# Gate products 44 steps later, sums of expert numbers on ScalarE, banks 4 and 4

## The chip, the cores and the metric

One core of a Trainium2 chip runs the kernel. The metric is the device time of one execution in microseconds (us). TensorE multiplies matrices, VectorE, ScalarE and GpSimd (POOL in the profile) work on 128 partitions at once, SyncE (SP) issues loads, and 16 DMA engines move the data. Each engine takes its own instructions in the order in which they were written out, and waits on semaphores for the others.

## The reference, cut to what matters

A decoder block on 512 tokens of 1024 features. A mixer (pooling heads, gating heads, one output projection) gives `x`. Then comes the expert part, for each token:

```python
s1, i1 = top_k(scores of key half 0, 16);  s2, i2 = top_k(scores of key half 1, 16)   # 8 heads
cv, ci = top_k(s1[:, None] + s2[None, :], 16)
expert = i1[ci // 16] * 128 + i2[ci % 16]            # 8 heads x 16 = 128 experts of 16384
gate   = softmax(cv)
act    = gelu(h2 . peer_u[expert])                   # 128 numbers
out    = sum over the 128 of gate * act * peer_v[expert]
```

The result is `rmsnorm(x + out)`.

## The kernel before, in words

The tokens are four tiles of 128. The *search* for expert numbers runs in groups A (tile 0), B (tile 1) and C (tiles 2 and 3), head by head: `q_unit` and `score` on TensorE, `top_keys` and `top_pairs` on VectorE, `numbers` on POOL (it multiplies a 0/1 mask with the candidate numbers into the tile `ml`, 50 candidates x 16 picks, one buffer per pool), and `collect`, which sums `ml` over the 50 candidates into `ef`, one nonzero each, and for A and B copies the 16 numbers to `eG`. Group C has two tiles in one `ml`.

Tiles 0 and 1 are then computed by *gather steps*: 512 steps (`g_step`), 128 over rows of `peer_u` and 128 over rows of `peer_v` for each of the two tiles. POOL issues an indirect DMA of 128 rows (0.5 MB, tile `ga`, NG = 6 buffers), VectorE multiplies: L401 forms a dot product per token into `actG`, L408/L410 add a weighted row. After 64 steps of the first kind ScalarE takes the Gelu of 64 columns (L404) and VectorE multiplies with the gates (L405) at once.

Tiles 2 and 3 are computed densely by TensorE over all 16384 experts: 128 `u_block`s (a block of `uT`, 0.5 MB, read by SyncE into five `raw` buffers; 16 matmuls into a PSUM bank "act"; evacuated by ScalarE with Gelu, L703, into `gl`), then 128 `v_block`s, which add into four banks over the rows of `peer_v`. In between the gates are spread over the experts: `hot_pieces` (VectorE), `spread` (TensorE) and `weigh` (VectorE) for two halves of 32. PSUM has eight banks: six named "bank" and two "act".

At the end `x_load` reads `norm_final` and the rows of x back into the room of the first `gl`, `total` adds, ScalarE sums squares, and `finish` normalizes and stores, once for each tile.

The order of all this is made by a planner in Python before anything is issued: `Plan.run` keeps a clock for each engine, and gives it the ready item of the lowest `prio`; an item has a cost in us and dependences with a delay. What `q_unit`, `score` and `u_block` ask of ScalarE is written out together with their TensorE item. Gather steps come when the list PACE allows, at prio 2 when they are due (one per SLOW us until SLOW_UNTIL, with `due` counted on from the first step) and at prio 4 otherwise; the search of A, B, C on VectorE has prio 1, 1.5 and 3. The planned times fix only the order of each engine's instructions; nothing waits for a clock on the chip.

Of the kernel before, what the change touches and what calls it, by code (L numbers as in the profile page):

```python
# [8 lines left out]
F32 = mybir.dt.float32  # L9
BF16 = mybir.dt.bfloat16  # L10
I32 = mybir.dt.int32
U32 = mybir.dt.uint32
AF = mybir.ActivationFunctionType
OP = mybir.AluOpType
# [4 lines left out]
P = 128  # L19
# [25 lines left out]
C_MM = 0.86  # L45
C_Q0, C_Q1, C_U, C_V, C_SMM = 2.1, 5.4, 3.43, 3.43, 1.5
C_HOT, C_MUL, C_GAT = 2.2, 0.72, 1.31
PACE = ((0.0, 1.85), (570.0, 2.12), (800.0, 1.98), (840.0, 2.12), (1050.0, 1.98), (1270.0, 1.4))
SLOW, SLOW_UNTIL = 2.9, 570.0
SLACK, SLIP, LAG = 8.0, 10.0, 6.0  # L50


# [93 lines left out]
def hybrid_block(ctx, tc, A):  # L146
# [4 lines left out]
    def bcast(ap, n):  # L151
        return bass.AP(tensor=ap.tensor, offset=ap.offset, ap=[[0, P], [1, n]])
# [9 lines left out]
        return keep.tile(shape, dt, name=name)  # L162

    def bank(shape):
        return psum[-1].tile(shape, F32, name="bank", bufs=6 if len(psum) > 1 else 3)

    def side_bank(shape, name, n):
        return psum[0].tile(shape, F32, name=name, bufs=n)
# [82 lines left out]
    def qt(shape, dt, name, **k):  # L251
        return mp.tile(shape, dt, name=name, **k)
# [2 lines left out]
    keysT = qt([P, 2, P], F32, "keysT")  # L255
    ident = qt([P, P], F32, "ident")
    iock = qt([P, NCAND, TOPK], BF16, "iock")
    ef, cv = {}, {}
    for g in "AB":
        ef[g] = qt([P, 1, HEADS, TOPK], F32, "ef" + g)  # L260
# [97 lines left out]

    def collect(g, h):
        ml = sums.pop((g, h))  # L360
        V.tensor_reduce(ef[g][:, :, h], ml.rearrange("p t c k -> p t k c"), AX.X, OP.add)  # L361
        if g != "C":
            V.tensor_copy(eG[:, TILES[g][0], h * TOPK:(h + 1) * TOPK], ef[g][:, 0, h])

    def softmax(g, gate):
        qt, n = kq(g), len(TILES[g])
# [20 lines left out]
    def gather(k):  # L387
# [2 lines left out]
        G.indirect_dma_start(out=ga[k], out_offset=None, in_=A["peer_v" if v else "peer_u"],  # L390
                             in_offset=bass.IndirectOffsetOnAxis(ap=eG[:, t, col:col + 1], axis=0))

    def g_step(k):
        while gissued[0] < min(k + NG, NSTEP):
            gather(gissued[0])
            gissued[0] += 1
        g = ga.pop(k)
        t, v, col = place(k)
        c = actG[:, t, col:col + 1]
        if not v:  # L400
            V.scalar_tensor_tensor(scr, g, 1.0, h2nat[t], op0=OP.mult, op1=OP.mult, accum_out=c)  # L401
            if col % HALF == HALF - 1:
                cs = slice(col + 1 - HALF, col + 1)
                S.activation(actG[:, t, cs], actG[:, t, cs], AF.Gelu)  # L404
                V.tensor_mul(actG[:, t, cs], actG[:, t, cs], gG[:, t, cs])  # L405
        elif col == 0:
            xe[t] = keep.tile([P, D], F32, name="h2n%d" % t)
            V.tensor_scalar(xe[t], g, c, None, op0=OP.mult)  # L408
        else:
            V.scalar_tensor_tensor(xe[t], g, c, xe[t], op0=OP.mult, op1=OP.add)  # L410
# [264 lines left out]
    gl, gp1, late = [None, None], [], {}  # L675

    def act_bank(shape):
        return psum[-1].tile(shape, F32, name="act", bufs=2)

    def switch():  # L680

# [115 lines left out]

    xr = {}

    def x_load():  # L800
        room = gp1[0].tile([P, HALF, GW], F32, name="gl1").rearrange("p a w -> p (a w)")
        for k, t in enumerate(("g", 0, 1, 2, 3)):
            xr[t] = room[:, k * D:(k + 1) * D]
            nc.scalar.dma_start(xr[t], bcast(A["norm_final"], D) if t == "g" else xd[t])

    def total(t):
        y = xr[t]
# [23 lines left out]
    def search(g, q, extra, prio):  # L831

        n = len(TILES[g])
        sc, tk, tp, nb, co = [], [], [], [], []
        for h in range(HEADS):
            sc.append(add("pe", 0.6 * n, lambda h=h: score(g, h), [(q[2 * h + 1], 0.8)] + extra, 2))
        back = 1 if g == "C" else 2
        for h in range(HEADS):
            tk.append(add("dve", 3.1 * n, lambda h=h: top_keys(g, h),
                          [(sc[h], 0.8)] + tp[-1:] + (nb[h - 2:h - 1] if h > 1 else []), prio))  # L840
            tp.append(add("dve", 2.6 * n + 0.2, lambda h=h: top_pairs(g, h),
                          [tk[-1]] + (nb[h - back:h - back + 1] if h >= back else []), prio))
            nb.append(add("pool", 1.5 + 1.5 * n, lambda h=h: numbers(g, h),
                          [(tp[-1], LAG)] + co[-1:], 1))
            co.append(add("dve", 1.5 * n + 0.1, lambda h=h: collect(g, h), [(nb[-1], 2.0)],
                          prio - 0.2))
        return sc, co, co[-1]

    q0 = []
# [26 lines left out]
    for r in range(2):  # L876
        hots, spreads, weighs = [], [], []
        for q in range(GW // SG):
            deps = hots[-1:] + spreads[-2:-1] + [us[(r + 1) * HALF - 1], late_item]
            if r:  # L880
                deps += [us[-1], sc[0][-1]]
            for cost, fn in hot_pieces(r, q):
                hots.append(add("dve", cost, fn, deps, 1.9))
                deps = hots[-1:]
            deps = [(hots[-1], SLACK)] + spreads[-1:] + [(w, 4.0) for w in weighs[-2:-1]]
            spreads.append(add("pe", C_SMM, spread, deps, 1))
            weighs.append(add("dve", C_MUL, weigh, [(spreads[-1], 2.0)] + weighs[-1:], 1.8))
        sc[r] = weighs
# [14 lines left out]
        marks[n] = Item("dve", 0.0, None)  # L903
        return marks[n]

    xl = add("act", 0.3, x_load, [(vs[HALF], 2.0)], 1)
    for t, last in enumerate((steps_end(2 * P), steps_end(4 * P), vs[-1], vs[-1])):
        tot = add("dve", 1.4, lambda t=t: total(t), [(last, 0.3), (xl, 15.0)], 1.5)
        add("dve", 2.4, lambda t=t: finish(t), [(tot, 1.4)], 1.6)
# [66 lines left out]
```

## Time and profile before

| | |
|---|---|
| median of 3 runs | 1350.66 us (1347.7 to 1353.95) |
| profiled execution, its own time | 1349.46 us |
| its span, first to last instruction | 1347.7 us |
| mean granted TensorE clock | 0.966 |
| moved by DMA | 455.99 MB, mean 338 GB/s |

The span is that of the recorded instructions; 1.76 us of the execution lie around it. Busy times are shares of the span; idle time of an engine that isn't the bottleneck costs nothing. In a timeline, the bracket behind a row is the engine's idle time before it and what ended it.

### The profile page before, as it was taken

The page shows a single profiled execution, that of the slowest core. Times are in us where ns is not written, and L with a number is a line of the kernel's source. Part 1 is how long each engine was busy: PE and PEld are TensorE (multiplying, and loading weights), DVE is VectorE, ACT ScalarE, POOL GpSimd, SP SyncE. Part 2 cuts the span into 40 slices and gives each one's busy share as a digit, 9 for nine tenths or more (in the row PEclk, how much of TensorE's full clock was granted, in tenths as well). Part 3 has the DMA queues.
Part 4 walks back from the last instruction along what each step waited for, and adds up shares of the span by engine and source line. Part 5 has one row for each costly group of instructions (what it writes and reads, how often), then busy time and mean ns, then how long its engine had stood idle before and what let it go on. Part 6 is the DMA issues. An engine that isn't in the chain of part 4 may idle for free.

```text
span 1347.7 us, 17430 instructions
## 1 busy us (share of the span) xinstructions
PE 1249.9 (93%) x5998; PEld 843.3 (63%) x5998; DVE 1083.0 (80%) x2432; ACT 136.0 (10%) x314; POOL 701.2 (52%) x762
## 2 busy tenths in 40 slices
PE   6999986999999999999999997999999998999980
PEld 3485542899888888788888884544444443444430
DVE  2267887899899993799999996999999847566577
ACT  2311321111211111201010000000000000000001
POOL 0023376645776662755655664555656535444452
PEclk9999988999999999999999999999999999899995
DMA  9767269936799997899999999999999999999994
GB/s 348 277 228 261 81 216 399 349 103 210 276 383 357 369 350 266 331 372 381 386 400 358 400 349 410 353 382 392 404 372 406 391 410 367 406 409 410 409 383 183
DMA packets 127784, 455.99 MB, mean 338 GB/s; under 512 B 14288, under 2 KB 16720, under 8 KB 127696
## 3 DMA queue, kind: packets, MB, share of 16 engines
q0 software_dynamic: 74304, 270.57, 52.5%
q1 hardware_dynamic: 52240, 180.12, 35.6%
q10 hardware_dynamic: 1152, 4.19, 0.8%
q8 instruction: 47, 0.77, 0.2%
q14 instruction: 41, 0.34, 0.1%
HBM read 450.63 MB, written 4.19 MB: 337 GB/s over the span
## 4 chain that ended last, share of the span: by engine, by line
DMA 26%; PE 25%; DVE 19%; issue 18%; POOL 10%; ACT 1%; SPq 0%; POOLq 0%; DVEq 0%; another core or an unknown queue 0%; ACTq 0%
DMA ga<-peer_v,eG 18%; PE act L204 15%; POOL ga L390 8%; PE bank L204 8%; DMA ga<-peer_u,eG 7%; DVE h2n L410 5%; DVE scr L401 3%; DVE og L767 2%; DVE ob L762 1%; DMA raw<-w_in 1%; DVE gl L796 1%; PE g L204 1%; PE pb L204 1%; DVE oa L771 1%; DVE efA L361 1%
## 5 line engine op out<-in xcount | busy, mean ns | idle before, releaser
L204 PE MATMUL bank<-raw,gl 128*128 128x512 f32 x1024 | 452.6, 601 | 6.3 <-DMA raw<-peer_v 6.3
L204 PE MATMUL act<-h2T,raw 128*128 128x256 f32 x2048 | 452.5, 381 | 3.4 <-ACT gl L703 2.9
L390 POOL DMA_INDIRECT ga<-peer_v,eG x256 | 288.8, 1128 | 264.7 <-DVE h2n L410 180.8
L204 PEld LDWEIGHTS act<-h2T,raw 128*128 128x128 f32 x2048 | 387.3, 191 | 56.6 <-ACT gl L703 3.7
L390 POOL DMA_INDIRECT ga<-peer_u,eG x256 | 304.6, 1190 | 205.6 <-DVE scr L401 146.8
L410 DVE SCALAR_TENSOR_TENSOR h2n<-ga,actG,h2n 128x1024 f32<-128x1024 f32 x254 | 326.3, 1284 | 105.9 <-DMA ga<-peer_v,eG 100.6
L401 DVE SCALAR_TENSOR_TENSOR scr<-ga,h2n 128x1024 bf16<-128x1024 f32 x256 | 318.9, 1246 | 40.8 <-DMA ga<-peer_u,eG 34.8
L204 PEld LDWEIGHTS bank<-raw,gl 128*128 128x128 f32 x1024 | 194.3, 192 | 240.9 <-issue 233.0
L703 ACT ACTIVATE gl<-act 128x256 f32<-128x256 f32 x128 | 49.0, 384 | 419.0 <-PE act L204 355.8
L204 PE MATMUL pb<-raw,xs 128*128 128x512 f32 x192 | 86.7, 607 | 2.3 <-ACT gu L500 1.2
L204 PEld LDWEIGHTS <-ob 128*128 128x128 bf16 x1536 | 56.1, 98 | 37.7 <-issue 18.2
L356 POOL TENSOR_TENSOR ml<-eq,ce 128x800 f32<-128x800 bf16 (+1 forms) x24 | 49.2, 2049 | 55.0 <-DVE efA L361 29.9
L767 DVE TENSOR_TENSOR og<-oa,gT 128x512 bf16<-128x512 bf16 x192 | 73.7, 421 | 2.2
L204 PEld LDWEIGHTS pb<-raw,xs 128*128 128x128 f32 x192 | 37.0, 196 | 46.6 <-issue 42.7
L204 PE MATMUL bank<-h2T,raw 128*128 128x256 f32 x256 | 57.9, 379 | 0.0
L204 PEld LDWEIGHTS bank<-h2T,raw 128*128 128x128 f32 x256 | 47.4, 190 | 5.8
L762 DVE TENSOR_TENSOR ob<-iota,abT 128x1024 bf16<-128x1024 bf16 x64 | 43.9, 686 | 0.4 <-remote 0.4
L204 PE MATMUL g<-raw,xs 128*128 128x512 f32 x64 | 32.8, 657 | 10.5 <-DMA raw<-w_in 10.5
L204 PE MATMUL act<-og,ob 128*128 128x64 bf16 x768 | 30.6, 196 | 9.5 <-DVE og L767 6.8
L327 POOL TENSOR_TENSOR ce<-xf 128x8 f32<-128x8 f32 (+8 forms) x168 | 36.8, 253 | 2.0
L609 POOL DMA_DIRECT2D xd<-x x4 | 2.4, 608 | 62.1 <-DVE x L604 62.0
L204 PE MATMUL bank<-og,ob 128*128 128x64 bf16 x768 | 29.4, 193 | 4.3 <-DVE og L767 3.7
(173 smaller groups left out, 780.9 us busy)
## 6 DMA issues: line engine op xcount, KB each, us to landing
raw<-uT SPq DMA_DIRECT2D x128, 512.0 KB
raw<-peer_v SPq DMA_DIRECT2D x128, 512.0 KB
raw<-w_q SPq DMA_DIRECT2D x32, 512.0 KB
raw<-w_in SPq DMA_DIRECT2D x23, 512.0 KB
raw<-w_out SPq DMA_DIRECT2D x16, 512.0 KB
ga<-peer_u,eG POOLq DMA_INDIRECT x256
ga<-peer_v,eG POOLq DMA_INDIRECT x256
x<-x SPq DMA_DIRECT2D x4, 512.0 KB
```

The costliest lines, as they stand in the source:

```text
L204: T.matmul(out, l, r, start=start, stop=stop)
L327: eng.tensor_tensor(ov, av, bv, op=OP.add)
L356: G.tensor_tensor(ml, eq, ce[:, :, :, None].to_broadcast(sh), op=OP.mult)
L361: V.tensor_reduce(ef[g][:, :, h], ml.rearrange("p t c k -> p t k c"), AX.X, OP.add)
L390: G.indirect_dma_start(out=ga[k], out_offset=None, in_=A["peer_v" if v else "peer_u"], in_offset=bass.IndirectOffsetOnAxis(ap=eG[:, t, col ...
L401: V.scalar_tensor_tensor(scr, g, 1.0, h2nat[t], op0=OP.mult, op1=OP.mult, accum_out=c)
L410: V.scalar_tensor_tensor(xe[t], g, c, xe[t], op0=OP.mult, op1=OP.add)
L703: S.activation(gl[r][:, i], b, AF.Gelu)
L762: V.tensor_tensor(tl["b"], iota2[:, None].to_broadcast(sb), col(abT[:, 1, t]).to_broadcast(sb), op=OP.is_equal)
L767: V.tensor_tensor(tl[k], tl["a"], col(gT[:, k, t]).to_broadcast(sa), op=OP.mult)
L771: V.tensor_tensor(tl["a"], iota2[:, None, r * HALF:(r + 1) * HALF].to_broadcast(sa), col(abT[:, 0, t]).to_broadcast(sa), op=OP.is_equal)
L796: V.tensor_mul(x, x, b.rearrange("p t a -> p a t"))
```

## The change

- The product with the gates leaves the step that takes the Gelu: `gate_half(t, 0)` comes at step 108 over `peer_u` (the Gelu is at step 63), `gate_half(t, 1)` at step 44 over `peer_v` (the Gelu is 45 steps earlier).
- `collect` is 16 ACTIVATEs with an accumulator output for each tile on ScalarE, instead of one reduction on VectorE; the copy to `eG` goes to ScalarE as well. The planner has it as an item of ScalarE of 4 us a tile, 4 us after `numbers`.
- "bank" has four buffers and "act" four. A `spread` is planned after the `weigh` three before it rather than two.
- The five loads of `x_load` become five items, eight `v_block`s apart, in the order norm, 0, 2, 3, 1.
- PACE, SLOW: other numbers.

```diff
@@ -45,8 +45,8 @@
 C_MM = 0.86
 C_Q0, C_Q1, C_U, C_V, C_SMM = 2.1, 5.4, 3.43, 3.43, 1.5
 C_HOT, C_MUL, C_GAT = 2.2, 0.72, 1.31
-PACE = ((0.0, 1.85), (570.0, 2.12), (800.0, 1.98), (840.0, 2.12), (1050.0, 1.98), (1270.0, 1.4))
-SLOW, SLOW_UNTIL = 2.9, 570.0
+PACE = ((0.0, 1.85), (570.0, 2.1), (800.0, 2.02), (840.0, 2.1), (1050.0, 2.02), (1290.0, 1.5))
+SLOW, SLOW_UNTIL = 2.6, 570.0
 SLACK, SLIP, LAG = 8.0, 10.0, 6.0
 
 
@@ -162,7 +162,7 @@
         return keep.tile(shape, dt, name=name)
 
     def bank(shape):
-        return psum[-1].tile(shape, F32, name="bank", bufs=6 if len(psum) > 1 else 3)
+        return psum[-1].tile(shape, F32, name="bank", bufs=4 if len(psum) > 1 else 3)
 
     def side_bank(shape, name, n):
         return psum[0].tile(shape, F32, name=name, bufs=n)
@@ -255,6 +255,7 @@
     keysT = qt([P, 2, P], F32, "keysT")
     ident = qt([P, P], F32, "ident")
     iock = qt([P, NCAND, TOPK], BF16, "iock")
+    cj = qt([P, NCAND], BF16, "cj")
     ef, cv = {}, {}
     for g in "AB":
         ef[g] = qt([P, 1, HEADS, TOPK], F32, "ef" + g)
@@ -358,9 +359,11 @@
 
     def collect(g, h):
         ml = sums.pop((g, h))
-        V.tensor_reduce(ef[g][:, :, h], ml.rearrange("p t c k -> p t k c"), AX.X, OP.add)
+        for t in range(len(TILES[g])):
+            for k in range(TOPK):
+                S.activation(cj, ml[:, t, :, k], AF.Copy, accum_out=ef[g][:, t, h, k:k + 1])
         if g != "C":
-            V.tensor_copy(eG[:, TILES[g][0], h * TOPK:(h + 1) * TOPK], ef[g][:, 0, h])
+            S.activation(eG[:, TILES[g][0], h * TOPK:(h + 1) * TOPK], ef[g][:, 0, h], AF.Copy)
 
     def softmax(g, gate):
         qt, n = kq(g), len(TILES[g])
@@ -390,6 +393,10 @@
         G.indirect_dma_start(out=ga[k], out_offset=None, in_=A["peer_v" if v else "peer_u"],
                              in_offset=bass.IndirectOffsetOnAxis(ap=eG[:, t, col:col + 1], axis=0))
 
+    def gate_half(t, n):
+        cs = slice(n * HALF, (n + 1) * HALF)
+        V.tensor_mul(actG[:, t, cs], actG[:, t, cs], gG[:, t, cs])
+
     def g_step(k):
         while gissued[0] < min(k + NG, NSTEP):
             gather(gissued[0])
@@ -402,8 +409,12 @@
             if col % HALF == HALF - 1:
                 cs = slice(col + 1 - HALF, col + 1)
                 S.activation(actG[:, t, cs], actG[:, t, cs], AF.Gelu)
-                V.tensor_mul(actG[:, t, cs], actG[:, t, cs], gG[:, t, cs])
-        elif col == 0:
+            if col == 108:
+                gate_half(t, 0)
+            return
+        if col == 44:
+            gate_half(t, 1)
+        if col == 0:
             xe[t] = keep.tile([P, D], F32, name="h2n%d" % t)
             V.tensor_scalar(xe[t], g, c, None, op0=OP.mult)
         else:
@@ -675,7 +686,7 @@
     gl, gp1, late = [None, None], [], {}
 
     def act_bank(shape):
-        return psum[-1].tile(shape, F32, name="act", bufs=2)
+        return psum[-1].tile(shape, F32, name="act", bufs=4)
 
     def switch():
 
@@ -797,11 +808,14 @@
 
     xr = {}
 
-    def x_load():
-        room = gp1[0].tile([P, HALF, GW], F32, name="gl1").rearrange("p a w -> p (a w)")
-        for k, t in enumerate(("g", 0, 1, 2, 3)):
-            xr[t] = room[:, k * D:(k + 1) * D]
-            nc.scalar.dma_start(xr[t], bcast(A["norm_final"], D) if t == "g" else xd[t])
+    rows = ("g", 0, 2, 3, 1)
+
+    def x_load(k):
+        if k == 0:
+            xr["room"] = gp1[0].tile([P, HALF, GW], F32, name="gl1").rearrange("p a w -> p (a w)")
+        t = rows[k]
+        xr[t] = xr["room"][:, k * D:(k + 1) * D]
+        nc.scalar.dma_start(xr[t], bcast(A["norm_final"], D) if t == "g" else xd[t])
 
     def total(t):
         y = xr[t]
@@ -842,8 +856,7 @@
                           [tk[-1]] + (nb[h - back:h - back + 1] if h >= back else []), prio))
             nb.append(add("pool", 1.5 + 1.5 * n, lambda h=h: numbers(g, h),
                           [(tp[-1], LAG)] + co[-1:], 1))
-            co.append(add("dve", 1.5 * n + 0.1, lambda h=h: collect(g, h), [(nb[-1], 2.0)],
-                          prio - 0.2))
+            co.append(add("act", 4.0 * n, lambda h=h: collect(g, h), [(nb[-1], 4.0)], 2))
         return sc, co, co[-1]
 
     q0 = []
@@ -882,7 +895,7 @@
             for cost, fn in hot_pieces(r, q):
                 hots.append(add("dve", cost, fn, deps, 1.9))
                 deps = hots[-1:]
-            deps = [(hots[-1], SLACK)] + spreads[-1:] + [(w, 4.0) for w in weighs[-2:-1]]
+            deps = [(hots[-1], SLACK)] + spreads[-1:] + [(w, 4.0) for w in weighs[-3:-2]]
             spreads.append(add("pe", C_SMM, spread, deps, 1))
             weighs.append(add("dve", C_MUL, weigh, [(spreads[-1], 2.0)] + weighs[-1:], 1.8))
         sc[r] = weighs
@@ -903,7 +916,8 @@
         marks[n] = Item("dve", 0.0, None)
         return marks[n]
 
-    xl = add("act", 0.3, x_load, [(vs[HALF], 2.0)], 1)
+    for k in range(5):
+        xl = add("act", 0.3, lambda k=k: x_load(k), [(vs[HALF + 4 + 8 * k], 2.0)], 1)
     for t, last in enumerate((steps_end(2 * P), steps_end(4 * P), vs[-1], vs[-1])):
         tot = add("dve", 1.4, lambda t=t: total(t), [(last, 0.3), (xl, 15.0)], 1.5)
         add("dve", 2.4, lambda t=t: finish(t), [(tot, 1.4)], 1.6)
```

## Rows read from the trace of the kernel before

**Rows 1.** The page's first part: span, and busy time of each engine.

```profile
span 1347.7 us, 17430 instructions
PE 1249.9 (93%) x5998; PEld 843.3 (63%) x5998; DVE 1083.0 (80%) x2432; ACT 136.0 (10%) x314; POOL 701.2 (52%) x762
```

**Rows 2.** Windows by stage: length, busy by engine, clock, DMA share, GB/s.

```profile
242.00:371.00 129.00, 127.89 (x762) 116.95 (x762) 118.06 (x469) 23.68 (x48) 77.06 (x125) 1.00 0.67 232
371.00:573.00 202.00, 199.13 (x919) 174.77 (x918) 169.27 (x503) 25.92 (x64) 126.01 (x143) 0.99 0.91 343
...
505.00:573.00 68.00, 65.13 (x298) 56.82 (x297) 37.07 (x72) 10.97 (x25) 33.19 (x30) 0.98 0.80 300
...
573.00:1300.00 727.00, 706.37 (x3526) 427.16 (x3525) 603.99 (x866) 25.44 (x66) 396.00 (x347) 0.99 1.00 389
```

**Rows 3.** Timeline of VectorE at 536 us: start, duration, instruction.

```profile
535.89 0.22 DVE L405 TENSOR_TENSOR actG<-actG,gG 128x64 f32<-128x64 f32 x1 [22.95 <-ACT actG L404]
```

**Rows 4.** Timeline of ScalarE, 531 to 537 us.

```profile
535.33 0.38 ACT L703 ACTIVATE gl<-act 128x256 f32<-128x256 f32 x1 [3.07 <-PE act L204]
535.61 0.25 ACT L404 ACTIVATE actG<-actG 128x64 f32<-128x64 f32 x1
```

**Rows 5.** Timeline of TensorE, 560 to 1320 us: its three longest waits.

```profile
569.90 8.71 PE L204 MATMUL act<-h2T,raw 128*128 128x256 f32 x32 [2.87 <-ACT gl L703]
...
839.49 4.07 PE L204 MATMUL act<-og,ob 128*128 128x64 bf16 x48 [6.84 <-DVE og L767]
...
1147.99 160.82 PE L204 MATMUL bank<-raw,gl 128*128 128x512 f32 x368 [6.33 <-DMA raw<-peer_v]
```

**Rows 6.** Timeline of VectorE: totals of tile 1, then tiles 2, 3.

```profile
1329.37 1.22 DVE L813 TENSOR_TENSOR gl<-gl,h2n 128x1024 f32<-128x1024 f32 x1
...
1334.91 2.48 DVE L811 TENSOR_TENSOR gl<-gl,bank 128x512 f32<-128x512 f32 x4
```

**Rows 7.** Groups of instructions by line: the sums on VectorE; busy, mean ns.

```profile
L361 DVE TENSOR_REDUCE efC<-ml 128x32 f32<-128x1600 f32 x8 | 22.9, 2864 | 3.4 <-POOL ml L356 3.4
...
L361 DVE TENSOR_REDUCE efB<-ml 128x16 f32<-128x800 f32 x8 | 12.1, 1517 | 2.3 <-POOL ml L356 2.3
L361 DVE TENSOR_REDUCE efA<-ml 128x16 f32<-128x800 f32 x8 | 12.0, 1499 | 2.0 <-POOL ml L356 2.0
```

**Rows 8.** Windows of L401 (two records a step), then of L410 (one a step).

```profile
95.00:514.00 419.00, 163.22 (x256) 0.96 0.77 282
...
1300.00:1330.00 30.00, 26.81 (x21) 0.73 0.86 314
```

**Rows 9.** Groups by line: ScalarE's ACTIVATEs of 1024, 512 and 64 values.

```profile
L814 ACT ACTIVATE scr<-gl 128x1024 bf16<-128x1024 f32 x4 | 4.2, 1056 | 266.8 <-DVE gl L813 262.3 <-DVE gl L811 4.4
...
L529 ACT ACTIVATE junk<-gu 128x512 bf16<-128x512 f32 x4 | 2.5, 629 | 7.9 <-DVE gu L543 7.8
...
L404 ACT ACTIVATE actG<-actG 128x64 f32<-128x64 f32 x4 | 1.0, 254 | 247.8 <-DVE scr L401 247.8
```

**Rows 10.** Timeline of ScalarE at 146 us: ACTIVATEs with an accumulator output.

```profile
145.75 0.63 ACT L529 ACTIVATE junk<-gu 128x512 bf16<-128x512 f32 x1 [7.08 <-DVE gu L543]
146.29 0.19 ACT L529 ACTIVATION_READ_ACCUMULATOR junk<-gu 128x1 f32 x1
146.50 0.63 ACT L529 ACTIVATE junk<-gu 128x512 bf16<-128x512 f32 x1
```

**Rows 11.** Timeline of TensorE, queries of group A.

```profile
97.19 3.74 PE L204 MATMUL bank<-h2TA,raw 128*128 128x128 f32 x32
```

**Rows 12.** Timeline of TensorE, queries of groups B and C, two scores.

```profile
258.76 1.50 PE L204 MATMUL bank<-keysT,qT 128*128 128x128 f32 x12
...
270.58 1.50 PE L204 MATMUL bank<-keysT,qT 128*128 128x128 f32 x12
```

**Rows 13.** Who waited for whom: us in total, times, longest.

```profile
POOL ml L356 <- DVE efA L361: 29.9, 5, 12.1
```

**Rows 14.** Waits of SyncE's load queue, the same columns.

```profile
SPq L187 <- DMA out<-gl: 15.6, 1, 15.6
```

## The prediction

> **What bounds the kernel now.** First the page's totals: TensorE is busy 93% of the span [rows 1], which makes it look like the only bound. The windows by stage say more [rows 2]. From 242 to 371 us the queues moved 232 GB/s and VectorE was nearly full (118 of 129 us). From 371 to 573 us they moved 343 GB/s. From 573 to 1300 us they moved 389 GB/s at a DMA share of 1.00 with TensorE at 706 of 727 us. So after 573 us the transfers are the bound, with TensorE 3% behind, and whatever is gathered before 573 us need not be gathered after it. In that reserve there is one hole: the stretch 505 to 573 us moved only 300 GB/s.
>
> VectorE's timeline shows why: the product of L405 waited 22.95 us for ScalarE's Gelu of L404 [rows 3]. ScalarE's timeline shows that this Gelu ran at 535.61 us, right behind the evacuation of a `u_block` [rows 4]. ScalarE takes its instructions in the order written out, and evacuations are tied to TensorE; VectorE had run about 22 us ahead of TensorE and was made to wait. Six gathers were in flight; when they had landed, no more were asked for.
>
> The end: TensorE's last product ends at 1147.99 + 160.82 = 1308.8 us [rows 5], the last gather step ends at 1329.4 us [rows 6], and 18.3 us of sums, normalization and stores follow. The span is 1347.7 us, the profiled execution's own time 1349.46 us (1.76 us around it), which is 1.2 us under the median shown.
>
> **Gate products 44 steps later.** Each is 224 ns and stays on VectorE; what goes is the wait of 22.95 us. The Gelu now has some 45 steps (over 80 us at the pace of 1.85 to 2.6 us) before it is needed, more than VectorE's lead of 22 us.
>
> **The sums leave VectorE.** They took 12.0 + 12.1 + 22.9 = 47.0 us there [rows 7], all before 551 us. VectorE's freed time goes to gather steps through the planner: before 570 us a step is due once per SLOW, 2.9 us before and 2.6 us after. The Gelu stands at the planned place of 535 us after 128 steps [rows 3, 4], so the rule's zero lies at 535 - 128 x 2.9 = 164 us, and by 2.6 the same place has (535 - 164) / 2.6 = 143 steps: 15 more. They cost VectorE 15 x 163.22 / 128 = 19 us [rows 8], less than the 47.0 us freed. The queues can carry them: 371 to 573 us moved 202 x 343 = 69.3 MB, and at 389 GB/s it would be 78.6 MB, room for 17.7 gathers of 0.524 MB. I take 15; bounds 0 (the lead is lost again) and 20 (some also fit ahead of 371 us, where the queues were a third empty). After 573 us, 15 gathers are 7.9 MB at 389 GB/s: **-20 us** (0 to -27).
>
> The new PACE asks for fewer steps between 570 and 1290 us (348 instead of 353 by its numbers). The trace has 21 steps left at 1300 us [rows 8] where the plan, at 143 + 353 by 1290 us and one per 1.4 us after, has nine, so the transfers and not the plan set these steps; I count it as nothing. If the plan did bind, it would cost 5 x 1.35 = 7 us.
>
> **ScalarE's price.** The trace has no ACTIVATE over 50 strided values. From above: 254 ns for 64 values [rows 9] and 210 ns for the accumulator read (146.29 to 146.50 us, [rows 10]) are 0.46 us a pair. From below: a 512-value ACTIVATE gives way to its read after 0.54 us [rows 10], and 1024 against 512 values are 1056 against 629 ns [rows 9], 0.83 ns each, so 50 values take 0.54 - 0.385 = 0.155 us, and a pair 0.365 us. I take 0.38, near the lower end, because the instructions overlap in that row. A sum for one tile is 16 pairs, 6.1 us (5.8 to 7.4); for the two tiles of group C 12.2 us (11.7 to 14.8); in all 512 pairs, 195 us on an engine with 136 us of work now [rows 1]. The plan books 4 and 8 us, too little. A row of VectorE is 1.50 us for what I estimate at 6.1 [rows 7]. (The Trainium skill, "ScalarE: Activation LUTs", Rules for kernel authors, wants adds on VectorE rather than ScalarE. The rows agree on the engine times; by this rule alone the extra 4.6 us would stand on the path 16 times over groups A and B and 9.3 us 8 times over C, some 150 us. It is the last rival below carried to its end, 1349 + 150 = 1500 us, and gets no chance of its own: the trace has ScalarE 90% idle.)
>
> What queues behind a sum is the next evacuation on ScalarE, and behind that TensorE:
>
> - Group A, 75 to 107 us: two query units take 3.74 us [rows 11], and the next score needs the second one's copy one unit (1.8 us) later. A sum of 6.1 us can hold it back 0 to 4.3 us; two or three fall there. I take 8 us, as the 25 us around them leave TensorE no gap.
> - Queries of B and C, 242 to 337 us: one unit is 5.24 us, and a copy has one unit before the score at 270.58 us needs it [rows 12]. Six B sums cost 0 to 0.9 us each, two C sums 0 to 7 us each: I take 2 + 5.
> - `u_block`s, 338 to 560 us: an evacuation each 3.45 us [rows 4]. With two banks a sum of 12.2 us would stop TensorE for some 5 to 8 us; with the four `act` banks of the change there are 13.8 us. I take 2 for the places where a B and a C sum follow each other.
>
> That is +17 us. The four banks also remove the 2.87 us in which TensorE waited at 569.90 us for the evacuation [rows 5]: +14 us for TensorE (0 to 98, if every sum cost its most: 8 x 4.3 + 8 x 0.9 + 8 x 7). A later TensorE asks for its blocks later: 14 / 3.45 = 4 blocks of 0.524 MB fewer by 573 us, **+5 us** of transfer later. POOL waits too: `ml` has one buffer, and POOL already stood 29.9 us for VectorE's sums [rows 13]; gathers are behind it. I put this into the bound 0 of the head start.
>
> **Banks 4 and 4; weights one step looser.** The four accumulators still fit in `bank`; the second half of the `spread`s gets four `act` buffers instead of two. TensorE's waits for those were 1.3 us at most: nothing, bounds 0 and -2.
>
> **Final rows one at a time.** The five loads (2.6 MB, 6.7 us of transfers) remain; bytes don't change. SyncE's load queue waited 15.6 us for the store of the first finished row, and TensorE stood 6.33 us for a `peer_v` block then [rows 5, 14]. The store comes later, but nothing takes the wait out. 0 in the sum, -6 as bound.
>
> **Sum.** Steps end: 1329.4 - 20 + 5 = 1314 us. TensorE's end: 1308.8 + 14 = 1323 us less what the lighter queues give back of its waits after 573 us (6.84 and 6.33 us are the two large ones, [rows 5]), so 1310 to 1323 us. Both meet near 1315 us. With the steps last, 18.3 us follow; with TensorE last only the totals of tiles 2 and 3 and what is behind them, 1347.7 - 1334.9 = 12.8 us [rows 6]. 1315 + 18.3 = 1333 us, + 1.76 = **1335 us**, 1.1% under the profiled execution. Its own range is 1326 to 1343 us.
>
> **Rivals.**
>
> - *Hidden sums, more head start.* TensorE loses 3 us instead of 14 and 20 steps are gained: 1349.5 - 27 + 1 - 3 = 1320 us (1310 to 1326). For it: ScalarE's 136 us. Against: it drains in order.
> - *The wait comes back.* VectorE and POOL can't lead, since POOL's next `ml` waits for a sum that stands in ScalarE's order behind TensorE's evacuations; the 22.95 us are spent in gathers queued behind POOL. Head start 0 to 5 steps: 1349.5 - 0 to 7 + 5 = 1343 to 1355, say 1348 us. For it: the lead of 22 us itself, and that ScalarE's order made the wait of before. Against: six gathers of cover.
> - *ScalarE stops TensorE (slower).* Each C sum holds a query copy or, queued behind a B sum, fills four banks. TensorE's end plus 12.8 us decides when 1308.8 + d - 10 + 12.8 passes 1354.4, so from d = 43 us; with 8 C sums at 7 us and half of A's, d = 73 us and the time is 1308.8 + 73 - 10 + 12.8 + 1.8 = 1386 us; at half of that d, 1350. I name 1370 us. For it: the plan's 4 us against 6.1. Against: slack of a unit, and four banks.
>
> **Chances.** Forecast 0.45, hidden 0.20, wait back 0.18, TensorE stopped 0.17. A difference under 0.5% (6.8 us) can't be told from none here. Faster holds the forecast and the hidden case: 0.65. Same is the wait's return and a little of the stop: 0.17. Slower: the rest, 0.18. The range leaves out the far half of the stopped case and the tail of the hidden one: 1312 to 1360 us.
>
> **What would show it.** Right: no wait at the gate products; 150 or more steps by 573 us and more than 300 GB/s in 505 to 573; sums of about 6 and 12 us in ScalarE's row; last gather near 1314. Wrong: idle time of TensorE for ScalarE's `qT` or `gl` copies of over 40 us before 573; POOL standing at `ml` for ScalarE with VectorE waiting for `ga`; fewer than 145 steps at 573 us.

## The result, and the profile after

| | before | after |
|---|---|---|
| median | 1349.18 us | 1381.9 us (4 runs, 1380.66 to 1383.27) |
| span of the profiled execution | 1347.7 us | 1380.5 us |
| TensorE's last product ends | 1308.8 us | 1369.6 us |
| VectorE's last gather step ends | 1329.4 us | 1306.1 us |

The change is slower: ratio 1.0253, 95% interval 1.0229 to 1.0277. The forecast was 1335 us in a range to 1360, so it had the wrong sign. Two ends moved in opposite directions: the gather steps end 23 us earlier, and TensorE ends 61 us later.

The page's first part, for the kernel after (before: [rows 1]):

```profile
span 1380.5 us, 18464 instructions
PE 1265.3 (92%) x5998; PEld 851.0 (62%) x5998; DVE 1044.9 (76%) x2392; ACT 326.1 (24%) x1354; POOL 691.9 (50%) x762
```

ScalarE gained 190 us of work (326.1 - 136.0), and VectorE lost 38. Now the windows by stage of the same kernel, with the columns of [rows 2]:

```profile
242.00:371.00 129.00, 106.19 (x633) 97.46 (x634) 98.30 (x405) 76.71 (x339) 65.18 (x111) 0.90 0.59 211
371.00:573.00 202.00, 200.77 (x919) 174.45 (x918) 174.58 (x548) 116.57 (x550) 137.65 (x168) 0.99 0.95 359
505.00:573.00 68.00, 66.77 (x309) 57.66 (x308) 51.41 (x97) 40.20 (x185) 46.97 (x49) 1.00 0.96 369
573.00:1300.00 727.00, 681.39 (x3538) 430.79 (x3537) 615.99 (x885) 29.32 (x76) 401.49 (x353) 0.97 1.00 389
```

The third row is what the change was to bring: 369 instead of 300 GB/s between 505 and 573 us. The first is the loss: between 242 and 371 us TensorE issued 633 products instead of 762, with 76.7 us of ScalarE instead of 23.7. The last one has a second loss: TensorE was busy 681 of 727 us, before 706.

TensorE's timeline shows where; the bracket is the idle time before the row and what ended it (before: [rows 5]):

```profile
107.69 3.53 PE L204 MATMUL bank<-h2TA,raw 128*128 128x128 f32 x16 [3.24 <-ACT qT L278]
...
328.94 2.97 PE L204 MATMUL bank<-h2TB,raw 128*128 128x128 f32 x16 [3.40 <-ACT qT L286]
...
352.00 0.49 PE L204 MATMUL bank<-keysT,qT 128*128 128x128 f32 x2 [3.38 <-ACT sc L297]
...
368.31 2.50 PE L204 MATMUL bank<-keysT,qT 128*128 128x128 f32 x10 [6.97 <-ACT eG L366]
370.61 1.91 PE L204 MATMUL act<-h2T,raw 128*128 128x256 f32 x4
...
1121.76 151.29 PE L204 MATMUL bank<-raw,gl 128*128 128x512 f32 x348 [3.98 <-DVE gl L807]
...
1298.80 70.83 PE L204 MATMUL bank<-raw,gl 128*128 128x512 f32 x160 [25.75 <-DMA raw<-peer_v]
```

The first `u_block` (`act<-h2T`) starts at 370.61 us; before it was 338.28. Of these 32.3 us, 12.8 are there by the first query of B (255.70 us, before 242.94); the other 19.6 come between that query and the first `u_block`. In the waits of TensorE up to 371 us, those for ScalarE sum to 33.1 us, before to 5.5. Near the end there is one wait of 25.75 us for a block of `peer_v`, where the kernel before had one of 6.33 us.

What ScalarE did ahead of the first of these waits, in its timeline:

```profile
100.52 0.28 ACT L278 ACTIVATE qT<-bank 128x128 f32<-128x128 f32 x1 [1.46 <-PE bank L204]
100.70 0.28 ACT L364 ACTIVATE cj<-ml 128x50 bf16<-128x50 f32 x1
100.88 0.19 ACT L364 ACTIVATION_READ_ACCUMULATOR cj<-ml 128x1 f32 x1
101.10 0.29 ACT L364 ACTIVATE cj<-ml 128x50 bf16<-128x50 f32 x1
...
107.03 0.19 ACT L364 ACTIVATION_READ_ACCUMULATOR cj<-ml 128x1 f32 x1
107.25 0.22 ACT L366 ACTIVATE eG<-efA 128x16 int32<-128x16 f32 x1
107.37 0.26 ACT L278 ACTIVATE qT<-bank 128x128 f32<-128x128 f32 x1
```

A sum holds ScalarE from 100.70 to 107.37 us without a gap: 16 pairs at 0.41 us each and the copy of the numbers. Units of queries take 1.8 us here, so the `qT` copy at 107.37 had been due some five us earlier; TensorE's next query product starts 0.3 us after it. The stop costs more than its idle time: the 16 products behind it took 3.53 us, where 16 take 1.95 a little earlier, and from 107 to 112 us the granted clock was 0.66 (before: 1.00).

Among the queries of B, sums that stood alone were hidden, and a run of them was not. Two more windows of the same kernel:

```profile
256.00:325.00 69.00, 69.00 (x443) 64.10 (x442) 58.02 (x278) 29.15 (x131) 32.52 (x65) 1.00 0.58 209
325.00:371.00 46.00, 31.44 (x168) 28.22 (x167) 27.96 (x102) 40.53 (x197) 25.11 (x39) 0.85 0.51 172
```

In the first, two sums of B (from 295.81 and from 307.57 us) took nothing from TensorE. From 315.37 to 367.54 us two sums of C and three of B then followed each other, with under 3 us between them, and in the second window TensorE was busy 31.4 of 46 us.

And what held the load at the end. First the waits of SyncE's load queue (us in total, times, longest; before: [rows 14]), then ScalarE's timeline with the stores of rows 0 and 1:

```profile
SPq L187 <- DMA out<-gl: 41.3, 2, 35.0
```

```profile
1285.91 0.34 ACTq L834 DMA_DIRECT2D out<-gl  x1
...
1311.77 0.34 ACTq L834 DMA_DIRECT2D out<-gl  x1
```

A load of SyncE's queue stood 35.0 us until a store of a finished row had landed, and all loads behind it stood too. Such a store waits for VectorE. In the trace, the transfers of SyncE and ScalarE take eight completion semaphores in turn (101, 103 to 107, 109 and 110): row 0's store has 105, and the load that stood 35.0 us waited for 105. So a load whose turn falls on the semaphore of an open store waits for that store. Before, row 0's store went out at 1136 us and row 1's after the last load; now they come at 1286 and 1312 us, with loads still to issue.

The four products with the gates, of which one is shown, have no wait at all any more (before: [rows 3]), and the last step on VectorE ends 23 us earlier than in [rows 6]:

```profile
606.22 0.22 DVE L398 TENSOR_TENSOR actG<-actG,gG 128x64 f32<-128x64 f32 x1
...
1304.79 1.28 DVE L421 SCALAR_TENSOR_TENSOR h2n<-ga,actG,h2n 128x1024 f32<-128x1024 f32 x1 [1.25 <-DMA ga<-peer_v,eG]
1306.11 1.23 DVE L827 TENSOR_TENSOR gl<-gl,h2n 128x1024 f32<-128x1024 f32 x1
```

So there are two suspects for the time. **S**: the sums stand in ScalarE's queue ahead of the copies that TensorE needs. **L**: SyncE's load queue stands behind the late store of a finished row.

### The profile page after: what moved, and what is told of

Its sections match the earlier page's. It is cut to its first block, busy times and chain, and to the rows that moved or that the text cites. A ratio compares the mean times of both kernels' runs of the same rounds, so it can differ in the third digit from the quotient of the medians.

```text
span 1380.5 us, 18464 instructions
## 1 busy us (share of the span) xinstructions
PE 1265.3 (92%) x5998; PEld 851.0 (62%) x5998; DVE 1044.9 (76%) x2392; ACT 326.1 (24%) x1354; POOL 691.9 (50%) x762
## 4 chain that ended last, share of the span: by engine, by line
PE 32%; DMA 23%; DVE 21%; issue 12%; ACT 7%; POOL 5%; SPq 0%; DVEq 0%; POOLq 0%; ACTq 0%
PE act L204 13%; DMA ga<-peer_v,eG 13%; PE bank L204 13%; DVE h2n L421 8%; DMA ga<-peer_u,eG 6%; ACT cj L364 5%; PE pb L204 5%; POOL ga L393 4%; DVE scr L408 4%; DVE og L778 3%; DVE ob L773 2%; DMA raw<-w_in 2%; DVE gl L807 1%; DVE oa L782 1%; DMA swT<-sgu_wT 1%
## 5 line engine op out<-in xcount | busy, mean ns | idle before, releaser
L204 PE MATMUL bank<-raw,gl 128*128 128x512 f32 x1024 | 453.6, 602 | 29.7 <-DMA raw<-peer_v 25.7
L421 DVE SCALAR_TENSOR_TENSOR h2n<-ga,actG,h2n 128x1024 f32<-128x1024 f32 x254 | 330.7, 1302 | 103.5 <-DMA ga<-peer_v,eG 96.1
L393 POOL DMA_INDIRECT ga<-peer_v,eG x256 | 293.9, 1148 | 226.2 <-DVE h2n L421 163.2
L393 POOL DMA_INDIRECT ga<-peer_u,eG x256 | 296.9, 1160 | 192.8 <-DVE scr L408 122.9
L364 ACT ACTIVATE cj<-ml 128x50 bf16<-128x50 f32 x512 | 147.1, 287 | 19.8 <-POOL ml L357 4.4
L364 ACT ACTIVATION_READ_ACCUMULATOR cj<-ml 128x1 f32 x512 | 95.8, 187 | 0.0
L204 PE MATMUL pb<-raw,xs 128*128 128x512 f32 x192 | 89.7, 624 | 6.1 <-ACT gv L511 4.9
L828 ACT ACTIVATE scr<-gl 128x1024 bf16<-128x1024 f32 x4 | 4.2, 1057 | 323.1 <-DVE gl L827 262.4
```

The costliest lines, as they stand in the source:

```text
L204: T.matmul(out, l, r, start=start, stop=stop)
L364: S.activation(cj, ml[:, t, :, k], AF.Copy, accum_out=ef[g][:, t, h, k:k + 1])
L828: S.activation(scr, y, AF.Square, accum_out=fin[:, t:t + 1])
```

## The experiments

**Undoing the sums, and a first try at the stores (e1 to e4).** e1 is the changed kernel with `collect` on VectorE; e2 writes the stores of rows 0 and 1 out after the last product; e3 does both; e4 is the kernel before with the sums on ScalarE alone.

```
e1, e3:  V.tensor_reduce(ef[g][:, :, h], ml..., AX.X, OP.add)
         V.tensor_copy(eG[...], ef[g][:, 0, h])
         co.append(add("dve", 1.5 * n + 0.1, ..., [(nb[-1], 2.0)], prio - 0.2))
e2, e3:  add("act", 0.3, lambda t=t: store(t), [fi, vs[-1]], 1)      # t < GT
```

> The changed kernel with the sums of expert numbers back on VectorE (reduction, cast and planner item as before); all else stays changed. Theory S (the sums queue in ScalarE ahead of TensorE's evacuations): the first u_block starts near 340 us instead of 370.6 us, and the time falls by about 30 us, to 1345 to 1355 us. Theory L (SyncE's load queue behind the store of a finished row is what costs): the 25.75 us of TensorE waiting for a peer_v block stay, and the early delay was hidden by the transfers anyway, so the time stays within 8 us of 1381.9 us.

> The changed kernel with the stores of rows 0 and 1 issued only after the last v_block, so that no load comes behind them. Theory S alone: the time moves by under 5 us, as loads would then wait for something else. Theory L: SyncE's wait of 35 us for out<-gl and TensorE's 25.75 us are gone, and the time falls by 20 to 26 us, to about 1358 us. The first u_block still starts near 370 us in both.

> Both edits together: sums on VectorE and the stores at the end; what is left of the change is the later gate products, banks 4 and 4, the split loads and the pace. If S and L are separate losses that add, the time is about 1381.9 - 30 - 24 = 1328 us, faster than before. If they are the same loss, it equals the better of the other two, about 1350 us.

> The kernel before with only the sums moved to ScalarE (function and planner item as in the change, two act banks and six others, old pace, old gate products). Theory S: the first u_block starts 20 to 35 us later than 338 us and the time rises by 15 to 35 us. Theory L: the sums by themselves cost under 7 us.

| | median us | ratio to before (95%) | first `u_block` | SyncE's waits for a store |
|---|---|---|---|---|
| e1 | 1368.25 | 1.0154 (1.0127 to 1.018) | 338.3 | 31.3 |
| e2 | 1380.45 | 1.025 (1.0222 to 1.0278) | 369.6 | 34.2 |
| e3 | 1362.16 | 1.0113 (1.0084 to 1.0141) | 335.7 | 16.9 |
| e4 | 1440.75 | 1.0684 (1.065 to 1.0717) | 370.6 | 52.8 |

e1 and e3 give the whole delay of the first `u_block` back, so S is right for that stretch, and e4 shows that the sums alone make it. But e1 gains only 14 us, between what the two theories expected: a wait of 12.7 us for a `peer_v` block stays, and another wait appeared in TensorE's timeline (e1):

```profile
338.26 7.07 PE L204 MATMUL act<-h2T,raw 128*128 128x256 f32 x32
...
580.70 1.09 PE L746 MATMUL bank<-ident,af 128*128 128x128 f32 x4 [21.26 <-DVE af L738]
```

The transposes of the gates wait for VectorE, which is late with the search of group C: with SLOW 2.6 the plan gives it more gather steps there, and the sums are on it again. With the old pace (e6, below) this wait is gone. e2 says nothing of L, because its edit did not take the store out of the loads' way: row 0's store, now behind row 1's sum of squares on ScalarE, left at 1308 us, and a load with 13 more behind it stood 34.2 us for the same semaphore, 101. By the order written out this store comes behind the last load; the turns of the semaphores don't follow that order.

e4 rose by 94 us where 15 to 35 were expected. Its two `act` banks of before meet 13 us sums; its waits of TensorE, us in total, times, longest:

```profile
PE act L204 <- ACT gl L706: 44.2, 9, 8.9
PE bank L204 <- DMA raw<-peer_v: 29.7, 2, 23.9
PE bank L204 <- ACT qT L286: 15.7, 4, 8.9
```

In the changed kernel the first of these is absent. Its four `act` banks are the likely reason; no run changes only the banks of e4.

**The stores behind the last load, and three subsets (e5 to e8).** The stores of rows 0 and 1 now go out on SyncE's own queue, behind its last load, so that no load can stand behind them. e5 is the changed kernel with this; e6 has the sums on VectorE and the old pace besides; e7 is the kernel before with the gate products 44 steps later; e8 is e5 with the sums of A and B on VectorE and only those of C on ScalarE.

```
e5, e6, e8:  def store(t):
                 nc.sync.dma_start(A["out"][t * P:(t + 1) * P], xr[t])
             add("act", 0.3, lambda t=t: store(t), [fi, vs[-1]], 1)  # t < GT
e8:          if g == "C": ...ScalarE's loop...
             else: V.tensor_reduce(...); V.tensor_copy(...)
```

> The changed kernel, but the stores of all rows go out on SyncE's queue behind its last load, so no load of a weight can stand behind a store that waits for VectorE. L (SyncE's load queue stands behind the late store of a finished row): the 35 us wait of SyncE for a store goes, TensorE's 25.75 us wait for a peer_v load near 1299 us goes, and the time falls from 1382 by 15 to 25 us, to 1357 to 1367. S alone (the sums in ScalarE's queue are the whole loss): no change, 1378 to 1384, with TensorE waiting for the same loads for another reason, the transfers themselves. Both: the first u_block still begins near 370 us.

> The changed kernel with the sums on VectorE again, the pace table and SLOW of before, and the stores on SyncE behind its last load: what is left of the change is the gate products 44 steps later, banks 4 and 4 and the split loads of the final rows. S and L with the pace as a third part (SLOW 2.6 packs steps ahead of search C): the first u_block begins near 338 us, the 21 us wait of TensorE at the transposes of the gates that the kernel with VectorE sums had goes to under 5 us, no load stands behind a store, and the time is 1325 to 1338. Rival T (transfers and VectorE's steps set the end of both kernels, as the last gather step ended at 1329 us before): 1343 to 1350, with the last step again at 1325 us or later.

> The kernel before with the gate products 44 steps later and nothing else. If the 22.95 us wait of VectorE for Gelu was worth what the prediction took it for, steps by 573 us rise by about 10 and the last step ends 15 to 20 us earlier, near 1312, while TensorE's end stays near 1309: 1333 to 1340. Rival T (the stall is caught up by later transfers anyway): the last step still ends near 1325 to 1329 and the time is 1345 to 1350.

> The changed kernel with the sums of groups A and B on VectorE and only those of group C on ScalarE, and the stores on SyncE behind its last load. S as worked out from the trace of after (the loss of 32 us falls ahead of the first u_block, in the mixer part of A and in the queries of B): the first u_block begins near 338 us, the sums of C (8 of 13 us on ScalarE) hold TensorE for 10 to 25 us between 390 and 560 us as its evacuations stand behind them, and the time is 1340 to 1355. If the sums hide in C, as the prediction had it for the u_blocks (2 us): 1328 to 1338. If the sums are as dear there as in A and B: 1360 or more.

| | median us | ratio to before (95%) | first `u_block` | TensorE ends | last step ends |
|---|---|---|---|---|---|
| e5 | 1357.25 | 1.0079 (1.0053 to 1.0105) | 370.1 | 1342.5 | 1319 |
| e6 | 1341.3 | 0.995 (0.9934 to 0.9965) | 335.3 | 1289.7 | 1317 |
| e7 | 1345.65 | 0.9969 (0.9953 to 0.9985) | 338.6 | 1306.2 | 1327 |
| e8 | 1339.09 | 0.9932 (0.991 to 0.9953) | 337.4 | 1312.5 | 1315 |

L holds: e5 stands at 1.0079 where the changed kernel stood at 1.0253, some 24 us, and TensorE has no wait for a load near the end. S holds for what is left: e8 differs from e5 in the sums of A and B alone and is 18 us faster, with TensorE's end 30 us earlier. The other 12 us don't show, because in e8 the steps and the 18 us behind them end last. Of e8, the first `u_block` came as expected; TensorE stood 6.5 us for `gl`, between the 2 and the 10 to 25 us of the two expectations, and so did the time. In it one sum of C falls alone among the queries (290 to 303 us), and they last 4.5 us longer than before. e6 came 3 us over what was expected of it: its last step ends 12 us earlier than before, with the same 18 us behind it.

e7 is the instructive miss: its time is that of the rival expectation, in which the stall is caught up anyway. The wait at the gate products is gone, but the steps by 573 us rise from 143 to 146, not by 10. VectorE's timeline, then ScalarE's (e7):

```profile
551.64 0.42 DVE L373 TENSOR_REDUCE sm<-cvC 128x16 f32<-128x256 f32 x1 [20.35 <-ACT cvC L370]
```

```profile
549.50 0.38 ACT L711 ACTIVATE gl<-act 128x256 f32<-128x256 f32 x1 [3.07 <-PE act L204]
549.90 1.28 ACT L370 ACT_TABLE_LOAD   x1
551.19 0.42 ACT L370 ACTIVATE cvC<-dl 128x256 f32<-128x256 f32 x1
551.63 1.28 ACT L711 ACT_TABLE_LOAD   x1
```

The stall of 22.95 us moved 16 us down the line and became one of 20.35: VectorE now waits for the exponential of C's softmax, which stands in ScalarE's order behind the evacuation of a `u_block`, just as the Gelu did. Both rows fit the same reading: VectorE has a lead over TensorE, and gives it back at the next place where it needs ScalarE. e6, with the sums back on VectorE, has the wait there too (18.6 us); in the changed kernel and e8 it is 0.5 us.

**A true price, the stores in the kernel before, the pace, the banks (e9 to e12).** e9 is e5 with the sums booked at 6.7 us a tile instead of 4.0; e10 the kernel before with e5's stores; e11 is e8 with the pace and SLOW of before; e12 the kernel before with banks 4 and 4 and the weights one step looser.

```
e9:   add("act", 6.7 * n, lambda h=h: collect(g, h), [(nb[-1], 4.0)], 2)
e11:  PACE, SLOW as before
e12:  bufs=4 if len(psum) > 1 else 3;  name="act", bufs=4;  weighs[-3:-2]
```

> The changed kernel with the stores on SyncE behind its last load (1357 us without more), and the plan books 6.7 us a tile for the sums on ScalarE, as measured, in place of 4.0. If the loss ahead of the u_blocks comes from the plan's false price (TensorE's units are written out so that each stands behind a sum that the plan thinks done): the first u_block begins at 345 to 358 us instead of 370, and the time falls to 1340 to 1350. If ScalarE's work itself is what holds them (it has to stand somewhere ahead of the last copy of the queries, and its queue drains in order): the first u_block stays at 362 to 374 us and the time at 1352 to 1360.

> The kernel before, with the stores of rows 0 and 1 on SyncE behind its last load and nothing else. L says what this wait is worth where TensorE isn't last: SyncE's 15.6 us and TensorE's 6.3 us go, but the gather steps end at about 1325 us as before, so the time is 1342 to 1349. If the load queue's wait costs as much in the kernel before as in the changed one (25 us): 1325 to 1335.

> The changed kernel with the sums of A and B on VectorE, those of C on ScalarE, the stores on SyncE behind its last load (1339 us so far), and the pace table and SLOW of before. If the pace of the change is what fills the stretch to 573 us with steps: 8 to 10 steps fewer by 573 us than its 156, the last step ends 8 to 12 us later, near 1327, and the time is 1344 to 1350. If the transfers and not the plan set the steps: 1336 to 1342.

> The kernel before with the banks divided 4 and 4 and the weights one step looser, and nothing else. The prediction counted this part at 0 to -2 us: 1345 to 1350, TensorE's waits for evacuations and weights at 570 us and after shorter by 3 to 4 us, and no effect on the last step. If six banks were needed (queries of C beside the u_blocks): waits of TensorE for ScalarE's qT or sc copies before 573 us of 5 us or more and 1350 to 1356.

e9: 1383.78 us, 1.0271 (1.0232 to 1.031). Of the second expectation the first `u_block` came, at 370.3 us: up to there the work itself holds TensorE, not its false price. The time fell outside both, 26 us over e5. The new loss is behind it. ScalarE's timeline, then TensorE's (e9):

```profile
448.39 0.28 ACT L364 ACTIVATE cj<-ml 128x50 bf16<-128x50 f32 x1 [0.92 <-POOL ml L357]
...
461.51 1.28 ACT L373 ACT_TABLE_LOAD   x1
462.81 0.31 ACT L373 ACTIVATE cvB<-dl 128x128 f32<-128x128 f32 x1
463.13 1.28 ACT L714 ACT_TABLE_LOAD   x1
464.43 1.21 ACT L714 ACTIVATE gl<-act 128x256 f32<-128x256 f32 x4
```

```profile
464.86 23.29 PE L204 MATMUL act<-h2T,raw 128*128 128x256 f32 x96 [4.35 <-ACT gl L714]
494.20 6.27 PE L204 MATMUL act<-h2T,raw 128*128 128x256 f32 x14 [6.05 <-ACT gl L714]
```

By the new order a sum of C (13.1 us) and the softmax of B (2.9 us) follow each other: 16.0 us in which no evacuation runs, against 4 x 3.45 = 13.8 us that four banks cover. The second stop begins with ScalarE itself waiting 6.00 us for POOL's `ml`. TensorE's idle time is only 10.4 us, but after the stops the granted clock in 450 to 573 us is 0.94, before them 1.00, and e5 has 1.00 throughout: 493 products in that stretch instead of 563. A share of 0.94 means that a part of it ran at 1.2 GHz and the rest at 2.4. At e5's 0.216 us a product, the 70 missing ones are 15 us; TensorE ends 28 us later than in e5, and the other 13 us go with longer waits for VectorE from 573 to 900 us (22.7 us, in e5 9.1). (The Trainium skill, "ScalarE: Activation LUTs", What ACT_TABLE_LOAD costs, counts about 2.66 us for every switch of tables. The rows above give 1.30 us from the load to the next ACTIVATE, so the two switches and the exponential take 2.9 us, where I estimate 5.6 from the page's figure.)

e10: 1344.34 us, 0.9973 (0.9947 to 0.9999), the last step at 1322 us: as expected, the load queue's wait is worth little where TensorE isn't last. e11: 1342.92 us, 0.997 (0.9948 to 0.9993), the last step at 1323 us: the new pace brings e8 some 4 us and not 10, with intervals that overlap. e12: 1348.45 us, 0.9998 (0.9976 to 1.002): banks and weights alone change nothing, as the prediction had it.

**Which part made the stores late (e13 to e17).** In the changed `x_load` loop the name `xl` ends as the last of five loads, and the totals of all rows wait for that one: the plan moves row 0's total from 1117 to 1241 us. Row 1's total moves from 1307 to 1268 us, since the plan's steps end earlier. e13 undoes the split in the changed kernel; e14 makes it in the kernel before; e15 is e13 with the sums of A and B on VectorE; e16 is the changed kernel with row 1's store alone on SyncE's queue, e17 the same without the split.

```
e13, e15, e17:  xl = add("act", 0.3, x_load, [(vs[HALF], 2.0)], 1)    # five loads at once
e14:            for k in range(5):
                    xl = add("act", 0.3, lambda k=k: x_load(k), [(vs[HALF + 4 + 8 * k], 2.0)], 1)
e16, e17:       if t == 1: add("act", 0.3, lambda t=t: store(t), [fi, vs[-1]], 1)   # nc.sync
```

> The changed kernel with the five loads of the final rows in one piece at the first product of the second half of v, as before; the stores stay where the change has them. If the split is what made the load queue's wait grow (R: the total of row 0 now waits for the last of five loads, at 1241 instead of 1117 us of the plan): SyncE's wait for the store of a row falls from 35 to 10 to 20 us and lies near 1150 us, where later loads can catch up, TensorE's wait for a peer_v load falls from 25.75 us to under 10, and the time from 1382 to 1358 to 1368. If the later TensorE or the earlier steps made it grow: 1376 to 1384, with the wait near 1299 us still 20 us or more.

> The kernel before with the final rows one at a time and nothing else. R: the store of row 0 comes after 1270 us, SyncE's queue stands behind it or behind that of row 1 for 25 us or more, TensorE gets a wait of 10 to 25 us near 1290 us, and the time is 1350 to 1372. If the prediction's step holds (nothing takes the wait out, nothing adds to it): 1345 to 1350, with TensorE's wait for a peer_v load at 6 us.

> The changed kernel with the two parts undone that the theories charge: the sums of A and B on VectorE, those of C on ScalarE, and the final rows' loads in one piece; the stores where they were. R and S together: the first u_block near 338 us, SyncE's wait for a store 10 to 20 us near 1130 us, and 1338 to 1350, all of the change's loss gone. If only the stores on SyncE's queue took the loss away and not the undone split: 1355 or more.

> The changed kernel with only the store of row 1 on SyncE behind its last load; row 0's store, which goes out near 1286 us, stays on ScalarE's queue. W (either of the two late stores is enough to stop the loads): SyncE's 35 us wait and TensorE's wait near 1299 us stay, 1375 to 1384. If row 1's store alone did it: 1355 to 1362.

> The same with the loads of the final rows in one piece as before, so that row 0's store goes out near 1168 us. W: the one store that is left on ScalarE's queue costs SyncE about 8 us near 1168 us, which later loads catch up; TensorE has no wait for a peer_v load over 7 us, and the time is 1355 to 1364. If the load queue's wait comes from elsewhere (TensorE late, lanes of other transfers): 1372 or more.

| | median us | ratio to before (95%) | stores on ScalarE's queue, rows 0, 1 | SyncE stands, longest | TensorE for `peer_v` near the end |
|---|---|---|---|---|---|
| e13 | 1381.19 | 1.024 (1.019 to 1.0291) | 1168, 1312 us | 34.0 | 20.7 |
| e14 | 1348.3 | 0.999 (0.9965 to 1.0016) | 1253, 1335 us | 39.5 | 29.7 |
| e15 | 1370.85 | 1.0153 (1.011 to 1.0195) | 1156, 1324 us | 37.4 | 24.3 |
| e16 | 1382.91 | 1.0249 (1.0201 to 1.0297) | 1291, none | 32.1 | 22.3 |
| e17 | 1356.61 | 1.0051 (1.003 to 1.0072) | 1175, none | 9.5 | none |

The split alone was not the cause: with it undone (e13) the load queue stands as long, for row 1's store instead of row 0's. SyncE's waits in e14 and e17:

```profile
SPq L187 <- DMA out<-gl: 39.5, 1, 39.5
```

```profile
SPq L187 <- DMA out<-gl: 9.5, 1, 9.5
```

Either of the two stores, if it is planned ahead of the last loads and comes late, is enough (e13, e16); only with both out of the way (e17, e5) do the 24 us come back. In the changed kernel they come later than planned: the plan has the last steps at 1266 us, the transfers of the chip end them at 1306. But a store need not be late against the plan: in e14 row 0's store is planned at some 1244 us and left at 1253, and a load had been standing for its semaphore since 1219. e14 also shows the split's own price: TensorE stands 29.7 us and ends 21 us later than before, at 1329.7, and the time doesn't change, since the steps end there too. e15's 1371 against e8's 1339 us is the same wait once more. e3, whose stores are written out as in e2, had only 16.9 us of it, and the two times make up the difference: its store left 13 us earlier (1294 against 1308 us), and the load came to wait for it 4 us later (1280 against 1276). Why a turn falls where it does is not settled.

## Why the prediction was wrong, by its steps

- **Gate products 44 steps later.** Right that the wait of 22.95 us goes in the changed kernel. It is right only together with the other parts: alone (e7) the wait returns as one of 20.35 us at C's softmax. The rival of the returning wait had a return of this kind, but at POOL's `ml`.
- **The sums leave VectorE: -20 us.** Near in size: 156 steps by 573 us against 143 before (15 more were forecast, 13 came), 369 GB/s in 505 to 573 us, and a last step at 1306 us, forecast 1314. In part that was luck. The plan itself has 179 steps by 573 us instead of 149, so 30 more and not the 15 of the forecast's rule, and e8, with the sums of A and B on VectorE, has 156 steps too. And the step at 1306 us goes with the loss at the end: in e5, where no load stands for a store, the last step ends at 1319 us.
- **ScalarE's price: +14 us for TensorE.** Mis-sized. The duration was nearly right: 0.41 us a pair for 0.38, 6.6 us a sum for 6.1, 13.1 for 12.2. What it does to TensorE was not: the first `u_block` came 32.3 us later, where A, B and C were to cost 8 + 2 + 5 = 15 ahead of it. A's sums, put at 75 to 107 us with a cost of 8, ran from 100.70 to 202.17 us, most of them beside the mixer, and cost 12.8. For B and C the forecast priced each sum by itself against one unit of slack (5.24 us). For a sum that stands alone that was about right: 0 for the two of B, 4.5 us for the one of C in e8, forecast 0 to 7. Ahead of the `u_block`s it had no term for sums that follow each other: five of them, from 315 to 368 us, held ScalarE 45.4 of 52.2 us, and the queries lost 19.6 us instead of 7. The waits for ScalarE grew by 27.6 us up to 371 us, and the granted clock in 242 to 371 us fell from 1.00 to 0.90, which no term held. Behind it, the four banks covered the sums as forecast; e9 shows how near to their 13.8 us this was.
- **Banks 4 and 4: 0.** Right by itself (e12). Beside the sums they are probably worth much: in e4, without them and without the rest of the change, TensorE waits 44.2 us for ScalarE's `gl`.
- **Final rows one at a time: 0, bound -6.** This is the step that failed in kind. It saw SyncE's wait of 15.6 us and said that "nothing takes the wait out"; it did not ask when the stores would now come, nor what loads would still be queued. The wait grew to 35.0 us and cost TensorE 25.75 us (e5: some 24 us of time). The half of it that e13 shows was to be had from the plan: it has row 1's total at 1268 us in place of 1307, while its last product ends at 1317 us (before 1315), so that this store now comes ahead of the last loads.
- **Sum.** TensorE's end was put at 1310 to 1323 us and came at 1369.6: +32.3 to the first `u_block`, +3.3 in the `u_block`s, and +25.2 in the rest (of it 25.75 - 6.33 = 19.4 for the load and 4.0 at 1121.76 us). Behind it lie 10.9 us, forecast 12.8. The signs that were named could not tell this: those for being right came or nearly came, and of those for being wrong one came in part (POOL stood 66.0 us at `ml` for ScalarE, before 29.9 for VectorE; TensorE's waits for ScalarE were 33.1 us, where over 40 were named). None was about TensorE or the loads after 573 us.
- **The rival "ScalarE stops TensorE"** had the right path, TensorE's end in place of the last step, and named 1370 us. Its threshold, a delay of about 43 us, was too high: 1354.4 us is about what the steps come to without any head start. In e5 TensorE is 34 us late and decides, 1342.5 + 10.8 us against 1319 + 18.3 for the steps. In the changed kernel the delay was 61 us, but little over half of it came from ScalarE, and that ahead of the `u_block`s, where only two of C's eight sums stood.

With the early sums on VectorE again and the stores out of the load queue's way, the kernel is 0.7% faster than before (e8: 0.9932, 0.991 to 0.9953). Moving the stores alone brings 0.9973 (e10), so the rest of the change is worth less than half a per cent.

## What to carry to other kernels

Work moved to an engine that is mostly idle is priced by the longest stretch in which that engine hardly answers anybody, blocks that follow each other counted together, against the slack of each consumer behind it; here 6.6 us alone cost nothing beside 5.2 us of slack, and a run of five sums cost 19.6 us. When a step is made earlier or later, follow every transfer that it issues, and ask what on the other queues gets to stand behind it: here a store that waited for VectorE belonged on the loads' own queue, behind the last of them. A stall that comes from one engine's lead over another moves to the next place where they meet.

## What the runs showed of the hardware that was not expected

- A store issued on ScalarE's queue held SyncE's loads for up to 39.5 us (e14), and the same store on SyncE's queue behind the last load held none (e5). (The Trainium skill, "DMA: Bandwidth & Descriptors", Issuing engines are not separate DMA queues, says that issuing transfers from several engines at once saves only the time that it takes to issue them. These runs show a second thing that the choice decides, the wait for a shared completion semaphore, some 24 us here.)
- An ACTIVATE of 50 values with its accumulator read takes 0.41 us from one to the next (0.287 and 0.187 us recorded, overlapping by 0.06).
